# An encoder trunk in split fp32: the up projections take their k-tiles outside and the two token tiles inside

## The chip, the cores and the metric

The kernel runs on one core of a Trainium2 chip. A core has several engines, each with an instruction stream of its own that it works through in order: TensorE (PE in the profile) multiplies matrices into eight PSUM banks, VectorE (DVE) and ScalarE (ACT) work element by element, GpSimd (POOL) does little here, and SyncE (SP) issues the transfers from memory. The metric is the device time of one execution in microseconds. Durations in this text are of the profiled execution unless a sentence says otherwise.

## The reference

The program is a bidirectional encoder of two layers over 256 tokens of width 1024, in fp32:

```python
def swiglu(h, w_gate, w_up, w_down):
    return (jax.nn.silu(h @ w_gate) * (h @ w_up)) @ w_down
...
    for layer in range(DEPTH):
        h = rms_norm(x, ffn1_norm[layer])
        x = x + 0.5 * swiglu(h, ffn1_w_gate[layer], ffn1_w_up[layer], ffn1_w_down[layer])
        h = rms_norm(x, mix_norm[layer])
        ...
        h = rms_norm(x, ffn2_norm[layer])
        x = x + 0.5 * swiglu(h, ffn2_w_gate[layer], ffn2_w_up[layer], ffn2_w_down[layer])
    return rms_norm(x, final_norm)
```

The inner width of a SwiGLU is 2816. The line left out adds a mixer, an attention layer of one of two kinds, which the change doesn't touch.

## The kernel before

**Stages.** The kernel goes through six stages: SwiGLU (stage 0), the even mixer (1), SwiGLU (2), SwiGLU (3), the odd mixer (4), SwiGLU (5). The 256 tokens are two token tiles of 128, and the width is eight k-tiles of 128. The activations of a stage lie transposed in SBUF as `hT[tt][k]`.

**One product.** An fp32 product is made of three passes over split operands. ACT writes the rounded `hi` of a weight piece (L479), DVE the rest `lo` (L482), and PE does high by `hi` (L471), high by `lo` (L472) and low by `hi` (L473) in `mm`. A piece is 128 x 512 weights. A split of two pieces (128 x 1024) lives in one of seven `wp` buffers until PE has used both pieces with both token tiles. Weights arrive in three `raw` buffers of 1 MB; the next transfer is issued when the `lo` of the last split of a raw buffer is made.

**A SwiGLU stage** goes through five chunks of 512 inner columns (ci0 to ci4), a mixed chunk of 256, and then the down projection. An ordinary chunk makes the gate G and then the up projection U. `project` (L602) does one token tile at a time: it takes one PSUM bank and runs through the eight k-tiles, then the other token tile does the same with the same pieces. After the first of them ACT applies `silu` out of the bank; after U, DVE multiplies in `glu` (L677), which is what empties the bank. The result is turned by a DMA transpose (ACT copies L556 and L560 around it) and split for the down projection.

**Seven chunks.** Some chunks (`SEVEN`: ci2 of stages 0 and 5, ci1 and ci3 of stages 2 and 3) make G and U together by a Strassen scheme for some pairs of k-tiles: seven products for eight, named "1", "00", "01", "7", "5", "10", "6" in the order of the program. Of the four pairs of k-tiles the first one or two are done plainly, and then three or two by the scheme. Product "1" is the first to take a `pj` bank, "5" takes the other one. The weights of such a pair need more work on DVE: sums `two`, sums within `raw` (L395), and two splits `shi`/`slo` that have three buffers of their own. After the last product "1", ACT copies its bank (L766), and DVE combines the products (L769 to L812).

**Banks.** PSUM has 2 `pj` banks, 3 `s`, 1 `o` and 2 `tp`. U of a chunk ahead of a seven chunk uses the two `pj` banks.

**Order.** Every engine's instructions run in the order in which the program emits them. A counter (`tick`, one per product) sets that order: each tick adds a rate (`RATE`, `AHEAD_RATE` in the chunk ahead of a seven chunk, `SEVEN_RATE` within) to what is due, and when a split is due and a buffer is free (`room`), its `hi` and `lo` are emitted there. Tasks such as `glu` and `silu` wait for a number of ticks. So a split that is supplied earlier stands ahead of a `glu` that is emitted later, in the order of DVE and ACT.

**Down projection.** `DOWN` gives the order of its pairs (p plain, s Strassen); the last two pairs of the list are held to the end. When the last s pair has been issued, `combine` (L932 to L953) adds its products to `x`, ten operations on DVE, and `ENDS` sets the rate and what is due from there. Then `add_to_x` (L614) adds the plain part, and the next stage's transposes (L527) read `x`.

Of the kernel before, what the change touches and what calls it, by code (L numbers as in the profile page):

```python
# [20 lines left out]
NT = 2  # L21
# [10 lines left out]
FF_CHUNKS = [512, 512, 512, 512, 512]  # L32
# [14 lines left out]
DOWN_RATE = {0: 1.24, 2: 1.38, 3: 1.32, 5: 1.2}  # L47
ENDS = {0: [0.43, 0], 2: [0.4, 1], 3: [0.34, 0], 5: [0.26, 2]}
EVEN_RATE = [0.38, 0.48, 0.48, 0.48, 0.5]
# [41 lines left out]
}  # L91
AHEAD_RATE = {
    0: 0.81,
    2: 0.62,
    3: 0.55,
    5: 0.6,
}
SEVEN_RATE = {
# [107 lines left out]
class Trunk:  # L206
# [395 lines left out]
    def project(self, hT, pieces, tag):  # L602
# [4 lines left out]
        return ps  # L607

    def add_to_x(self, tt, sl, ps, scale, last=True):
        nxt = self.next  # L610
        if nxt.n < 6:
            yield 1
        x = self.x[tt][:, sl.start : sl.start + ps.shape[-1]]
        self.nc.vector.scalar_tensor_tensor(x, ps, scale, x, op0=ALU.mult, op1=ALU.add)  # L614
        if last:
            self.after(tt, sl, nxt)
# [42 lines left out]
    def ffn(self):  # L659
# [5 lines left out]
        tasks = []  # L665
# [7 lines left out]

        def glu(tt, f0, w, u, s):
            yield 1
            m = self.t([P, 512], "glu", 3)
            nc.vector.scalar_tensor_tensor(m[:, :w], u[:, :w], self.now.r[tt], s[:, :w], op0=ALU.mult, op1=ALU.mult)  # L677
            self.spawn(transposed(tt, f0, w, m), GLU_WAIT)
# [45 lines left out]
        sevens = SEVEN[self.now.n]  # L724
# [130 lines left out]
        f0 = 0  # L855
        self.spawn(x_sums())
        for ci, w in enumerate(FF_CHUNKS):
# [5 lines left out]

            tags = ["pj", "s", "s", "pj"] if ci - 1 in sevens else ["s", "s", "pj", "pj"]
            G = self.take(KD)
            S = []
            if self.now.n + ci == 0:
                both = self.first_gates(G)
            for tt in range(NT):
                g = both[tt] if self.now.n + ci == 0 else self.project(self.ready(tt), G, tags[tt])  # L870
                S.append(self.t([P, 512], "silu", SILUS[self.now.n]))
                self.start(silu(tt, w, g, S[tt]))
            U = self.take(KD)
            for tt in range(NT):
                u = self.project(self.now.hT[tt], U, tags[NT + tt])
                tasks.append(self.start(glu(tt, f0, w, u, S[tt])))
            f0 += w // P
# [688 lines left out]
```

## Time and profile before

| | |
|---|---|
| median of 3 runs | 943.91 us (942.9 to 944.78) |
| profiled execution | 942.41 us, span 940.6 us, granted clock 0.999 |
| PE busy | 921.9 us (98%) |
| DVE busy | 782.9 us (83%) |
| ACT busy | 677.8 us (72%) |
| stage 0, stage 1 | 0 to 187 us, 187 to 277 us |
| stage 2, stage 3 | 277 to 457 us, 457 to 638 us |
| stage 4, stage 5 | 638 to 757 us, 757 to 940 us |

The span runs from the first to the last instruction. In a row of the timeline stand the start, the busy time, the engine, the line, the operation with out<-in, and in brackets the idle time of the engine just before it with what ended it. PE, DVE and ACT overlap one operation with the next, so the distance between two starts is what an operation costs in a row of them.

### The profile page before, as it was taken

What the parts mean: (1) busy time and instruction counts of PE and PEld (TensorE: products, weight loads), DVE (VectorE), ACT (ScalarE), POOL (GpSimd) and SP (SyncE); (2) the same over time, 40 slices, a digit from 0 to 9 for tenths busy, and PEclk for the clock granted to TensorE, in tenths of its full rate; (3) what the DMA queues carried; (4) which work ended last, traced back from release to release, by engine and by line L of the source; (5) the groups of instructions that cost most, each with busy time, mean ns of one, the idle gap of its engine ahead of it and who ended that gap; (6) DMA issues with size and microseconds to landing.
All of it is one profiled execution on the core that took longest, in us unless ns stands there. A gap on an engine that the chain in (4) does not pass through costs nothing.

```text
span 940.6 us, 12391 instructions
## 1 busy us (share of the span) xinstructions
PE 921.9 (98%) x4399; PEld 752.7 (80%) x4399; DVE 782.9 (83%) x1212; ACT 677.8 (72%) x1091; POOL 92.5 (10%) x152
## 2 busy tenths in 40 slices
PE   9999999999999999999999999999999999999997
PEld 6887888877878788888888878778878788878886
DVE  6799778778869989888978897999767687986997
ACT  7678975477787778875657778657877577768753
POOL 1300000064410000000100000008030000000001
PEclk9999999999999999999999999999999999999999
DMA  8857875554326577766467777565534458487761
GB/s 297 282 166 247 250 234 194 182 152 106 101 91 201 205 231 233 236 212 250 152 179 228 194 239 224 210 244 172 164 106 136 134 178 247 139 253 217 230 224 45
DMA packets 129343, 183.16 MB, mean 195 GB/s; under 512 B 50688, under 2 KB 63744, under 8 KB 129280
## 3 DMA queue, kind: packets, MB, share of 16 engines
q1 hardware_dynamic: 128704, 181.58, 60.9%
q8 instruction: 34, 0.56, 0.2%
q10 hardware_dynamic: 576, 0.79, 0.2%
q14 instruction: 29, 0.24, 0.1%
HBM read 169.76 MB, written 1.05 MB: 182 GB/s over the span
## 4 chain that ended last, share of the span: by engine, by line
PE 66%; DVE 16%; ACT 10%; DMA 4%; issue 3%; POOL 0%; SPq 0%; POOLq 0%; ACTq 0%; DVEq 0%
PE pj L471 9%; PE pj L472 9%; PE pj L473 9%; PE s L472 9%; PE s L473 9%; PE s L471 9%; DVE lo L482 7%; ACT hi L479 3%; DMA glu<-turned 2%; ACT turned L560 2%; DVE raw L395 2%; PE o L1040 2%; ACT shi L479 2%; PE tp L1117 1%; PE o L473 1%
## 5 line engine op out<-in xcount | busy, mean ns | idle before, releaser
L482 DVE TENSOR_TENSOR lo<-raw,hi 128x1024 fp32r<-128x1024 f32 (+1 forms) x372 | 375.9, 1030 | 80.8 <-ACT hi L479 79.3
L479 ACT ACTIVATE hi<-raw 128x1024 fp32r<-128x1024 f32 (+1 forms) x372 | 318.4, 889 | 49.9 <-PE pj L473 12.2
L471 PE MATMUL pj<-hi,th 128*128 128x512 f32 x367 | 146.7, 400 | 0.9 <-ACT glu L766 0.9
L472 PE MATMUL s<-lo,th 128*128 128x512 f32 x373 | 145.5, 390 | 0.9 <-DVE lo L482 0.7
L471 PE MATMUL s<-hi,th 128*128 128x512 f32 x373 | 146.2, 392 | 0.0
L472 PE MATMUL pj<-lo,th 128*128 128x512 f32 x367 | 143.9, 392 | 2.3 <-DVE lo L482 2.0
L473 PE MATMUL s<-hi,tl 128*128 128x512 f32 x373 | 145.3, 390 | 0.0
L473 PE MATMUL pj<-hi,tl 128*128 128x512 f32 x367 | 143.3, 390 | 0.0
L472 PEld LDWEIGHTS pj<-lo,th 128*128 128x128 f32 x367 | 69.1, 188 | 17.6 <-DVE lo L482 5.1
L472 PEld LDWEIGHTS s<-lo,th 128*128 128x128 f32 x373 | 70.0, 188 | 16.2 <-DVE lo L482 2.0
L473 PEld LDWEIGHTS s<-hi,tl 128*128 128x128 f32 x373 | 70.0, 188 | 14.6
L471 PEld LDWEIGHTS s<-hi,th 128*128 128x128 f32 x373 | 70.0, 188 | 14.3
L471 PEld LDWEIGHTS pj<-hi,th 128*128 128x128 f32 x367 | 69.0, 188 | 15.4 <-ACT glu L766 1.3
L473 PEld LDWEIGHTS pj<-hi,tl 128*128 128x128 f32 x367 | 68.9, 188 | 14.6
L491 POOL TENSOR_TENSOR rstd<-var,mhalf 128x1 f32<-128x1 f32 (+2 forms) x16 | 17.1, 1069 | 594.3 <-ACT th L512 315.3
L560 ACT COPY turned<-glu 128x1024 uint16<-128x1024 uint16 (+1 forms) x48 | 60.1, 1252 | 10.3 <-DMA glu<-turned 10.3
L556 ACT COPY turned<-glu 128x1024 uint16<-128x1024 uint16 (+1 forms) x48 | 46.3, 965 | 23.8 <-DVE glu L794 17.5
L479 ACT ACTIVATE shi<-raw 128x1024 fp32r<-128x1024 f32 x30 | 31.8, 1058 | 42.0 <-DVE raw L395 26.1
L471 PE MATMUL s<-hi,g_h 128*128 128x512 f32 (+1 forms) x131 | 51.3, 392 | 0.0
L473 PE MATMUL s<-hi,g_l 128*128 128x512 f32 (+1 forms) x131 | 50.9, 388 | 0.0
L472 PE MATMUL s<-lo,g_h 128*128 128x512 f32 (+1 forms) x131 | 50.8, 388 | 0.0
L482 DVE TENSOR_TENSOR slo<-raw,shi 128x1024 fp32r<-128x1024 f32 x30 | 36.7, 1222 | 9.9 <-ACT shi L479 9.5
(482 smaller groups left out, 1672.4 us busy)
## 6 DMA issues: line engine op xcount, KB each, us to landing
raw<-in_ffn_w_down SPq DMA_DIRECT2D x44, 1024.0 KB, 5.1
raw<-in_ffn_w_up SPq DMA_DIRECT2D x28, 1024.0 KB, 5.1
raw<-in_ffn_w_gate SPq DMA_DIRECT2D x26, 1024.0 KB, 5.2
raw<-in_ffn_w_gate SPq DMA_DIRECT2D x35, 512.0 KB, 3.9
raw<-in_ffn_w_up SPq DMA_DIRECT2D x32, 512.0 KB, 4.9
raw<-in_odd_w_qkv SPq DMA_DIRECT2D x12, 1024.0 KB, 5.8
raw<-in_even_w_in SPq DMA_DIRECT2D x4, 1024.0 KB, 5.0
raw<-in_even_w_out SPq DMA_DIRECT2D x8, 512.0 KB, 5.9
```

The lines of the kernel that those rows point to most:

```text
L395: add = lambda o, x, y: self.nc.vector.tensor_tensor(o, x, y, op=ALU.add)
L471: mm(ps, h, wh, start=first, stop=False)
L472: mm(ps, h, wl, start=False, stop=False)
L473: mm(ps, l, wh, start=False, stop=last)
L479: self.nc.scalar.activation(hi, src, AF.Copy)
L482: self.nc.vector.tensor_tensor(lo, src, hi.bitcast(F32), op=ALU.subtract)
L491: nc.gpsimd.tensor_tensor(r[:, :n], v[:, :n], self.mhalf[:, :n], op=ALU.pow)
L556: self.nc.scalar.copy(planes.rearrange("p (h c) -> p h c", h=2), back.rearrange("p (c h) -> p h c", h=2))
L560: self.nc.scalar.copy(planes.rearrange("p (c h) -> p h c", h=2), back.rearrange("p (h c) -> p h c", h=2))
L1040: self.nc.tensor.matmul(O[64 * s : 64 * s + 64, i * P : i * P + P], v(b0 + i, s, kc), pT[s][:, i, kc, :], start=(kc == 0), stop=(kc == 1),)
L1117: nc.tensor.transpose(tb[:, o : o + P], p[:, i, kc * P : kc * P + P], self.ident)
```

## The change

A new function `project_both` takes both PSUM banks at the start and runs over the k-tiles outside and the two token tiles inside, so that a weight piece is used with both token tiles at once, and both banks are complete only at the end. It is used for U of all ordinary chunks but ci4 and the chunk between two seven chunks (ci2 of stages 2 and 3), which is U of ci0, ci1 and ci3 in stages 0 and 5 and of ci0 in stages 2 and 3; and for G of ci1 and ci4 in stages 0 and 5 (G of ci0 in stage 0 was done that way before). The two `glu` tasks of such a U wait 1 and 3 ticks. `AHEAD_RATE` goes from 0.62, 0.55 and 0.6 to 0.7, 0.65 and 0.75 in stages 2, 3 and 5. In stage 3 the Strassen pair s6 of the down projection changes places with the plain pair p1, and what is due after it starts at 3 and not at 0.

```diff
-    3: "p0 p2 s5 s3 p4 s8 p10 p1 s6 p9 p7",
+    3: "p0 p2 s5 s3 p4 s8 p10 s6 p1 p9 p7",
...
-ENDS = {0: [0.43, 0], 2: [0.4, 1], 3: [0.34, 0], 5: [0.26, 2]}
+ENDS = {0: [0.43, 0], 2: [0.4, 1], 3: [0.34, 3], 5: [0.26, 2]}
...
-AHEAD_RATE = {
-    0: 0.81,
-    2: 0.62,
-    3: 0.55,
-    5: 0.6,
-}
+AHEAD_RATE = {0: 0.81, 2: 0.7, 3: 0.65, 5: 0.75}
...
+    def project_both(self, pieces, tags):
+        ps = [self.bank(tag) for tag in tags]
+        n = len(pieces)
+        for k in range(n):
+            for tt in range(NT):
+                self.mm(ps[tt], self.now.hT[tt][k], pieces[k], k == 0, k == n - 1)
+        return ps
...
-        def glu(tt, f0, w, u, s):
-            yield 1
+        def glu(tt, f0, w, u, s, wait=1):
+            yield wait
...
-            tags = ["pj", "s", "s", "pj"] if ci - 1 in sevens else ["s", "s", "pj", "pj"]
+            behind = ci - 1 in sevens
+            tags = ["pj", "s", "s", "pj"] if behind else ["s", "s", "pj", "pj"]
+            apart = ci + 1 == len(FF_CHUNKS) or behind and ci + 1 in sevens
             G = self.take(KD)
-            S = []
+            S, both = [], None
             if self.now.n + ci == 0:
                 both = self.first_gates(G)
+            elif ci and not behind:
+                both = self.project_both(G, tags[:NT])
             for tt in range(NT):
-                g = both[tt] if self.now.n + ci == 0 else self.project(self.ready(tt), G, tags[tt])
+                g = both[tt] if both else self.project(self.ready(tt), G, tags[tt])
                 S.append(self.t([P, 512], "silu", SILUS[self.now.n]))
                 self.start(silu(tt, w, g, S[tt]))
             U = self.take(KD)
+            both = None if apart else self.project_both(U, tags[NT:])
             for tt in range(NT):
-                u = self.project(self.now.hT[tt], U, tags[NT + tt])
-                tasks.append(self.start(glu(tt, f0, w, u, S[tt])))
+                u = both[tt] if both else self.project(self.now.hT[tt], U, tags[NT + tt])
+                tasks.append(self.start(glu(tt, f0, w, u, S[tt], 1 + 2 * tt if both else 1)))
```

After the change the lines of the file stand elsewhere: `hi`, `lo` and the three passes are L474, L477 and L466 to L468, `glu` is L680, the transpose's copies are L551 and L555, and `add_to_x` is L617.

The first place is DVE in stage 0, around the two `glu` of ci1, which empty the two `pj` banks that the seven chunk ci2 takes next. Before, the first of them (of bank `pj_104`) stands further up, and the second here, at its end:

```order
L395 TENSOR_TENSOR two_112_550<-raw_91_468 128x1024
L677 SCALAR_TENSOR_TENSOR glu_116_572<-pj_104_521,rstd_37_213,silu_92_472 128x512
L482 TENSOR_TENSOR g1_0_l_115_570<-turned_88_459,g1_0_h_114_569 128x512
L482 TENSOR_TENSOR lo_118_579<-raw_91_468,hi_117_578 128x1024
L395 TENSOR_TENSOR raw_91_468<-two_112_550,raw_91_468 128x512
L395 TENSOR_TENSOR raw_91_468<-raw_91_468 128x512
L482 TENSOR_TENSOR slo_120_588<-two_112_550,shi_119_587 128x1024
L482 TENSOR_TENSOR slo_122_598<-raw_91_468,shi_121_597 128x1024
L482 TENSOR_TENSOR lo_125_607<-raw_100_503,hi_124_606 128x512
L395 TENSOR_TENSOR two_126_613<-raw_100_503 128x1024
L677 SCALAR_TENSOR_TENSOR glu_132_628<-pj_113_565,rstd_48_258,silu_103_520 128x512
```

The same place on DVE after the change, where ci1's banks are `pj_104` and `pj_105`:

```order
L477 TENSOR_TENSOR slo_119_583<-raw_91_466,shi_118_582 128x1024
L477 TENSOR_TENSOR lo_124_595<-raw_99_501,hi_123_594 128x512
L390 TENSOR_TENSOR two_125_601<-raw_99_501 128x1024
L477 TENSOR_TENSOR g1_0_l_122_592<-turned_94_477,g1_0_h_121_591 128x512
L477 TENSOR_TENSOR lo_127_611<-raw_99_501,hi_126_610 128x1024
L390 TENSOR_TENSOR raw_99_501<-two_125_601,raw_99_501 128x512
L390 TENSOR_TENSOR raw_99_501<-raw_99_501 128x512
L477 TENSOR_TENSOR slo_129_623<-two_125_601,shi_128_622 128x1024
L680 SCALAR_TENSOR_TENSOR glu_134_633<-pj_104_519,rstd_37_213,silu_102_517 128x512
L680 SCALAR_TENSOR_TENSOR glu_135_641<-pj_105_520,rstd_48_258,silu_103_518 128x512
```

Both `glu` now stand behind the first Strassen pair of ci2 and most of the second; before, the first stood ahead of the first pair's own `slo`.

The second place is ACT at the end of the same seven chunk, from the copy of product "1" to the `hi` of the last pieces of G of ci3. Before:

```order
L766 ACTIVATE glu_162_755<-pj_138_664 128x512
L560 COPY turned_137_658<-glu_132_628 128x2x512
L704 ACTIVATE quarters_150_714<-turned_137_658 128x128
L479 ACTIVATE hi_165_770<-raw_144_690 128x1024
L479 ACTIVATE g1_4_h_167_778<-turned_137_658 128x384
L479 ACTIVATE hi_169_787<-raw_144_690 128x1024
```

The same place on ACT after the change:

```order
L769 ACTIVATE glu_159_748<-pj_137_661 128x512
L555 COPY turned_136_655<-glu_134_633 128x2x512
L704 ACTIVATE quarters_161_760<-turned_136_655 128x256
L474 ACTIVATE g0_4_h_162_762<-turned_136_655 128x512
L474 ACTIVATE hi_165_767<-raw_144_690 128x1024
L555 COPY turned_141_668<-glu_135_641 128x2x512
L707 ACTIVATE quarters_161_760<-turned_141_668 128x128
L474 ACTIVATE hi_167_780<-raw_144_690 128x1024
```

The work on the first token tile's turned result has moved down to here, and one `turned` copy now stands between the two `hi`.

The third place is DVE at the end of stage 3, from the held pairs' last `lo` to the first sum into `x` (bank `o`) that the next stage's transposes read. Before:

```order
L482 TENSOR_TENSOR lo_1362_5953<-raw_1343_5848,hi_1361_5952 128x1024
L482 TENSOR_TENSOR lo_1365_5971<-raw_1353_5897,hi_1364_5970 128x512 x2
L482 TENSOR_TENSOR lo_1367_5983<-raw_1353_5897,hi_1366_5982 128x512 x2
L482 TENSOR_TENSOR lo_1370_5997<-raw_1358_5925,hi_1369_5996 128x512 x2
L939 SCALAR_TENSOR_TENSOR x0_84<-pj_1306_5717,x0_84 128x512
L942 SCALAR_TENSOR_TENSOR silu_1372_6017<-tp_1318_5756,silu_1371_6011 128x512
L945 SCALAR_TENSOR_TENSOR glu_1373_6022<-tp_1311_5735,silu_1372_6017 128x512
L948 SCALAR_TENSOR_TENSOR silu_1374_6027<-s_1312_5739,silu_1372_6017 128x512
L936 TENSOR_TENSOR x0_84<-x0_84,silu_1374_6027 128x512
L953 SCALAR_TENSOR_TENSOR glu_1375_6033<-s_1312_5739,glu_1373_6022 128x512
L614 SCALAR_TENSOR_TENSOR x0_84<-o_1283_5617,x0_84 128x512
```

The same place on DVE after the change, where `combine` follows `lo_1365` directly, from the last of its first five operations on:

```order
L944 TENSOR_TENSOR x0_84<-x0_84,silu_1369_5989 128x512
L477 TENSOR_TENSOR lo_1372_5997<-raw_1353_5903,hi_1371_5996 128x512
L961 SCALAR_TENSOR_TENSOR glu_1370_5995<-s_1312_5739,glu_1368_5984 128x512
L477 TENSOR_TENSOR lo_1372_5997<-raw_1353_5903,hi_1371_5996 128x512
L944 TENSOR_TENSOR x1_85<-x1_85,glu_1368_5984 128x512
L944 TENSOR_TENSOR x1_85<-x1_85,glu_1370_5995 128x512
L477 TENSOR_TENSOR lo_1375_6020<-raw_1358_5925,hi_1374_6019 128x512 x2
L617 SCALAR_TENSOR_TENSOR x0_84<-o_1283_5617,x0_84 128x512
```

`combine` starts four `lo` earlier, but those four (of the odd mixer's weights) and the two sums into `x1` now stand ahead of the sum from bank `o`.

## The prediction

> **What bounds the kernel now.** I read the page's busy times first, then TensorE's waits, then VectorE around the seven chunks, then the chain of waits there.
>
> ```profile
> PE 921.9 (98%) x4399; PEld 752.7 (80%) x4399; DVE 782.9 (83%) x1212; ACT 677.8 (72%) x1091; POOL 92.5 (10%) x152
> ```
>
> PE is busy for 921.9 of 940.6 us and the change leaves its 4399 matmuls as they are. So a gain can only come out of 18.7 us, and what PE waits for by name is less (line, releaser, us in all, times, longest):
>
> ```profile
> PE tp L527 <- DVE x L614: 2.1, 1, 2.1
> PE pj L472 <- DVE lo L482: 2.0, 3, 0.9
> PE s L472 <- DVE slo L482: 0.9, 2, 0.4
> PE tp L472 <- DVE slo L482: 0.8, 1, 0.8
> PE s L472 <- DVE lo L482: 0.7, 2, 0.5
> ```
>
> Waits for weights (`lo`, `slo`) come to 2.0 + 0.9 + 0.8 + 0.7 = 4.4 us, and the end of stage 3 (L527) to 2.1. Of stage 0, the windows of U of ci1 and of the seven chunk ci2 show, after stretch and length, busy PE, PEld, DVE, ACT:
>
> ```profile
> 41.50:52.20 10.70, 10.70 (x49) 8.87 (x48) 6.89 (x8) 8.89 (x10) 3.26 (x12) 1.00 0.92 310
> 52.20:72.20 20.00, 20.00 (x90) 16.41 (x89) 19.50 (x23) 15.28 (x18) 0.00 (x0) 1.00 0.47 135
> ```
>
> DVE has 3.8 us free in U and 0.5 in the seven chunk; PE waits for none of it until G of ci3. A piece that is released after two products, not after the other token tile's eight, frees its buffer earlier, so DVE can work ahead in U. Whether that helps is in the chain of waits (start, us, engine, line):
>
> ```profile
> 61.15 0.24 PE pj L473
> 61.47 1.07 ACT shi L479
> ...
> 71.04 0.48 ACT glu L766
> 71.52 1.27 ACT turned L560
> ...
> 73.12 0.96 ACT hi L479
> ...
> 76.58 1.23 DVE lo L482
> 77.85 0.50 PE pj L472
> ```
>
> The wait at 77.85 goes back without a gap in DVE and ACT to 61.47, where a `shi` waits for PE: product "5" of the first pair frees its buffer. PE starts that chain. Work done sooner ahead of 61 us can't shorten it; a PE that comes later lengthens it.
>
> **The change, part by part.**
>
> *Stage 0, the bank.* U of ci1 now ends both banks at 52.4, and both `glu` stand on DVE behind the first Strassen pair and most of the second. Product "1" takes the first bank here:
>
> ```profile
> 57.82 0.39 PE L471 MATMUL pj<-hi,th 128*128 128x512 f32 x1
> ```
>
> When is that `glu` done? Prices on DVE are distances between starts:
>
> ```profile
> 46.53 1.23 DVE L482 TENSOR_TENSOR lo<-raw,hi 128x1024 fp32r<-128x1024 f32 x1 [2.22 <-ACT hi L479]
> 47.67 0.69 DVE L482 TENSOR_TENSOR g_l<-turned,g_h 128x512 fp32r<-128x512 f32 x1
> 48.28 0.69 DVE L482 TENSOR_TENSOR lo<-raw,hi 128x512 fp32r<-128x512 f32 x1
> 48.88 1.22 DVE L395 TENSOR_TENSOR two<-raw 128x1024 f32<-128x1024 f32 x1
> 50.01 0.74 DVE L677 SCALAR_TENSOR_TENSOR glu<-pj,rstd,silu 128x512 f32<-128x512 f32 x1
> 50.68 0.68 DVE L482 TENSOR_TENSOR g_l<-turned,g_h 128x512 fp32r<-128x512 f32 x1
> ...
> 52.41 0.68 DVE L395 TENSOR_TENSOR raw<-two,raw 128x512 f32<-128x512 f32 x1
> ...
> 53.74 1.22 DVE L482 TENSOR_TENSOR slo<-two,shi 128x1024 fp32r<-128x1024 f32 x1
> ```
>
> A wide `lo`, `slo` or `two` costs 1.14, a narrow `lo` or `g_l` 0.6, the two `raw` sums 1.33 (52.41 to 53.74), `glu` 0.67. The row at 46.53 had waited for its `hi`, and on ACT:
>
> ```profile
> 42.00 1.06 ACT L479 ACTIVATE hi<-raw 128x1024 fp32r<-128x1024 f32 x1 [3.15 <-DMA raw<-in_ffn_w_up]
> ...
> 44.88 0.67 ACT L672 ACTIVATE silu<-s,rstd 128x512 f32<-128x512 f32 x1
> 45.45 1.57 ACT L479 ACTIVATE hi<-raw 128x1024 fp32r<-128x1024 f32 x2
> ```
>
> The first of these `hi` waits for a transfer that isn't sooner now. Then come two `silu` (0.57 each) and the second `hi` (0.95), so that `lo` starts at 42.0 + 0.95 + 1.14 + 0.95 = 45.1. From there to the end of the first `glu` stand, by the order, `lo`, narrow `lo`, `two`, `lo`, sums, `slo`, `g_l`, `slo`, narrow `lo`, `two`, `g_l`, `lo`, sums, `slo`, `glu`: 8 x 1.14 + 4 x 0.6 + 2 x 1.33 + 0.67 = 14.85. The bank is free at 59.9, and **PE waits 2.1 us** at 57.82. Bounds: 1.1 if the `silu` don't stand in the way, 2.8 if a `shi` behind two turned copies on ACT holds DVE by 0.7 more. None of it is covered: all later products stand behind that one.
>
> *Stage 0, the way out.* The chain from 61.47 starts later by those 2.1, and its tail is longer. On ACT, from the copy (71.04), there now stand two turned copies and, besides, these:
>
> ```profile
> 65.28 0.42 ACT L701 ACTIVATE quarters<-turned 128x256 f32<-128x256 f32 x1
> 65.61 0.62 ACT L479 ACTIVATE g_h<-turned 128x512 fp32r<-128x512 f32 x1
> ```
>
> Copy 0.48, turned copy and its quarters 1.6 (71.52 to 73.12), `g_h` 0.5, `hi` 0.98, turned copy and quarters 1.6, `hi` 0.98, `lo` 1.27 make 7.4, against 6.8 (71.04 to 77.85) before: 0.6 more. Stage 0 loses 2.1 + 0.6 = **2.7 us** (1.7 to 3.4). The smallest of the three waits in the 2.0 us group, at most (2.0 - 0.93)/2 = 0.5 with the largest quoted below, lies in U of ci0; it may go, but the transfer at 42.0 sets the bank's time in either case, so nothing of it stays.
>
> A rule bears on this. DVE's rows show the first `glu` at 50.01, while PE still works into the other bank. The Trainium skill, "Perfetto Trace Analysis", section "Optimizing Tensor Performance", wants independent groups to rotate through banks so that emptying one overlaps the next group's matmuls. K outside gives that up for the two token tiles; were the overlap worth nothing, the sum would be 2.1 us lower here and 1.3 lower in stage 5.
>
> *Stage 5* has the same shape:
>
> ```profile
> 806.67 0.39 PE L471 MATMUL pj<-hi,th 128*128 128x512 f32 x1
> ...
> 826.84 0.50 PE L472 MATMUL pj<-lo,th 128*128 128x512 f32 x1 [0.93 <-DVE lo L482]
> ```
> ```profile
> 819.79 0.57 ACT L766 ACTIVATE glu<-pj 128x512 f32<-128x512 f32 x1
> ```
>
> In stage 0 U of ci1 began 16.3 us ahead of product "1" (41.50 to 57.82, 72 matmuls), so here at 790.3. Here the buffers limit how far DVE runs ahead: the seventh split after U's first needs that one's buffer, which is free after 12 matmuls, at 790.3 + 2.7 = 793.0. Then on DVE and ACT by turns: `hi` 0.95, `lo` 1.14, sums 1.33; on ACT `shi` 0.96, turned copy and quarters 1.6, narrow `hi` 0.5, `g_h` 0.5, turned copy and quarters 1.6, `g_h` 0.5, `hi` 0.96; on DVE `lo` 1.14, sums 1.33, `g_l` and small ones 1.0, `slo` 1.14, `glu` 0.67: 808.3, a wait of 1.6. Without that buffer's wait it is 0.8, and if DVE isn't held by ACT none; I take 1.3. The tail by the stage 0 prices is 7.4 against 826.84 - 819.79 = 7.05, so **1.7 us** (0 to 2.2).
>
> *Stages 2 and 3, seven chunks.* In stage 2 ci1 is the seven chunk, and before, the second `glu` of ci0 and a `g_l` ran here:
>
> ```profile
> 301.42 0.74 DVE L677 SCALAR_TENSOR_TENSOR glu<-pj,rstd,silu 128x512 f32<-128x512 f32 x1
> ...
> 312.24 0.68 DVE L482 TENSOR_TENSOR g_l<-turned,g_h 128x512 fp32r<-128x512 f32 x1
> ```
> ```profile
> 305.46 0.39 PE L471 MATMUL pj<-hi,th 128*128 128x512 f32 x1
> ...
> 319.44 0.50 PE L472 MATMUL tp<-slo,k14h 128*128 128x512 f32 x1 [0.79 <-DVE slo L482]
> ```
>
> Ahead of the first `glu` now stand a `slo`, a narrow `lo` and a `two` more than ahead of the second before (2.9), and one `glu` less (0.7): it ends at 302.1 + 2.2 = 304.3. Its bank is wanted at 305.5, so PE doesn't wait. The `g_l` of 312.24 moves behind the third pair's `two`; that is 0.6 more ahead of the `slo` that ends the wait at 319.44, less what starts sooner: **0.4 us** (-0.3 to 1.0; 2.9 if that `glu` slips past 305.5). In the other seven chunks DVE's order ahead of the waits is the same, or nothing waited: 0 (-0.5 to 0.5). The same holds for G of ci1 and ci4 and U of ci3, whose banks are long free: 0.
>
> *End of stage 3.*
>
> ```profile
> 605.67 4.63 DVE L482 TENSOR_TENSOR lo<-raw,hi 128x1024 fp32r<-128x1024 f32 x4
> ...
> 628.32 0.68 DVE L939 SCALAR_TENSOR_TENSOR x<-pj,x 128x512 f32<-128x512 f32 x1
> ...
> 632.16 0.68 DVE L614 SCALAR_TENSOR_TENSOR x<-o,x 128x512 f32<-128x512 f32 x1
> ```
> ```profile
> 632.89 0.66 PE L527 MATMUL tp<-mats,x 128*128 128x128 f32 x4 [2.06 <-DVE x L614]
> ```
>
> `combine` starts four `lo` earlier, but the sum from `o` stands behind all of it and two more `lo`. The second of the four `lo` ends at 607.9; s6 takes `lo`n, `two`, `lo`, sums, two `slo` = 6.5, and at 614.4 the last held pair's transfer is issued (5.1 in the page, so 619.6); two `hi`, then two `lo` end at 622.9; two narrow `lo` 1.2, and twelve operations of 0.64 ((632.16 - 628.32)/6) bring the sum to 631.7, **0.5 us** sooner, of which I count 0.4 (-0.6 to +1.5, later transfers or none).
>
> Sum: 2.7 + 1.7 + 0.4 - 0.4 = +4.4 us. The profiled execution has 942.4 (span 940.6 and 1.8 around it), so 946.8. It lies 1.5 below the median of the runs, 943.9, to which I add the same: **948.3 us**.
>
> **Rivals.**
> A, working ahead wins. If DVE reaches the first `glu` of stage 0 by 57.8, 2.1 us sooner than my sum, PE never waits for a bank, and with buffers that come free sooner the waits for weights (4.4) go; the longer tails stay (0.6 and 0.4): -3.4, 940.5. For it: 3.8 us of free DVE in U. Against: the chain at 61.47 starts at PE.
> B, it washes out: the first bank is waited for about 1 us in one stage, and the end of stage 3 pays for it: +0.5, 944.4. For it: every stall lies in work that the change doesn't remove.
> C, slower by more: the first `glu` of stage 2 slips too (2.9 in place of 0.4) and both stages wait at their upper ends (3.4 + 2.2): +8, 952. It decides once DVE is 1.1 us later there than my sum.
>
> **How the numbers follow.** Forecast 0.5, A 0.22, B 0.2, C 0.08. Its own range is 945.5 to 951; to hold the time 8 times in 10, with A and B, 940 to 951.5. What a measurement of this kernel can tell from no change is 0.2%, 1.9 us. Faster: A, 0.22. Same: B and a little of the forecast's low end, 0.22. Slower: 0.56.
>
> **What would show it.** A wait of PE for DVE's `glu` at product "1" of ci2 in stages 0 and 5, near 2 us and 1.3; the wait at G of ci3 still there, ended by `lo`, its chain starting at a PE product again; L527's wait near 1.6. No `glu` row among PE's waits, or G of ci3 without a stall, would make the prediction wrong; so would stage 2's stalls gone.

## The result: slower by 1%, the waits came where they were expected and longer

The changed kernel takes **952.05 us** (median of 4 runs, 951.21 to 954.12), the kernel before 943.4 in the same comparison (942.23 to 944.78): a ratio of 1.0096, 95% interval 1.0083 to 1.011. The forecast was 948.3 with a range up to 951.5, so the side was right and the loss, 9 us of span, about twice the 4.4 of the sum.

TensorE's work is the same. This is the row of busy times after the change; the span is 949.6 us, 9.0 more than before.

```profile
PE 922.1 (97%) x4399; PEld 752.2 (79%) x4399; DVE 786.4 (83%) x1212; ACT 676.3 (71%) x1091; POOL 91.9 (10%) x152
```

The view of PE's waits after the change (line, releaser, us in all, times, longest) has a new row at its head, `glu`, and the wait at the end of stage 3, now L522, is 0.3 shorter:

```profile
PE pj L466 <- DVE glu L680: 5.5, 2, 3.3
PE pj L467 <- DVE lo L477: 3.6, 5, 0.8
PE tp L522 <- DVE x L617: 1.8, 1, 1.8
PE s L467 <- DVE slo L477: 1.7, 3, 0.8
PE s L467 <- DVE lo L477: 1.5, 3, 1.1
```

The timeline of DVE after the change shows what stands ahead of the first `glu` in stage 0 (start, us, engine, line, out<-in, and in brackets the idle time before with what ended it):

```profile
44.60 1.83 DVE L477 TENSOR_TENSOR lo<-raw,hi 128x1024 fp32r<-128x1024 f32 x2 [0.84 <-ACT hi L474]
...
51.09 0.68 DVE L477 TENSOR_TENSOR g_l<-turned,g_h 128x512 fp32r<-128x512 f32 x1
52.77 1.23 DVE L477 TENSOR_TENSOR slo<-raw,shi 128x1024 fp32r<-128x1024 f32 x1 [1.00 <-ACT shi L474]
...
58.72 1.22 DVE L477 TENSOR_TENSOR slo<-two,shi 128x1024 fp32r<-128x1024 f32 x1
59.85 1.40 DVE L680 SCALAR_TENSOR_TENSOR glu<-pj,rstd,silu 128x512 f32<-128x512 f32 x2
```

and the timeline of PE shows who waits for it, product "1" of ci2 in stage 0 and in stage 5:

```profile
57.08 0.39 PE L468 MATMUL o<-hi,tl 128*128 128x512 f32 x1
60.74 0.47 PE L466 MATMUL pj<-hi,th 128*128 128x512 f32 x1 [3.28 <-DVE glu L680]
...
814.60 0.50 PE L466 MATMUL pj<-hi,th 128*128 128x512 f32 x1 [2.21 <-DVE glu L680]
```

U of ci1 is finished near 51.9, but the `glu` that empties its banks starts at 59.85, behind everything DVE was given first. PE takes its work in order, and everything later stands behind that product.

G of ci3 still stalls. The rows of ACT from the copy of product "1" on, and the two PE rows that end the stall:

```profile
73.97 0.57 ACT L769 ACTIVATE glu<-pj 128x512 f32<-128x512 f32 x1
74.44 1.35 ACT L555 COPY turned<-glu 128x1024 uint16<-128x1024 uint16 x1
...
76.67 1.05 ACT L474 ACTIVATE hi<-raw 128x1024 fp32r<-128x1024 f32 x1
77.62 1.32 ACT L555 COPY turned<-glu 128x1024 uint16<-128x1024 uint16 x1
...
79.03 0.50 PE L467 MATMUL pj<-lo,th 128*128 128x512 f32 x1 [0.75 <-DVE lo L477]
81.54 0.50 PE L467 MATMUL pj<-lo,th 128*128 128x512 f32 x1 [0.77 <-DVE lo L477]
```

In that G PE loses 2.22 us against the steady distance of 0.227 us between starts, where it lost 1.49 before; in stage 5 it is 2.21 against 1.64. In stage 2, 300 to 330 us, PE's waits were 0.8 (`slo`, into a `tp` bank) and 0.5 (`lo`) before; now the same view reads

```profile
PE s L467 <- DVE lo L477: 1.1, 1, 1.1
PE tp L467 <- DVE slo L477: 0.8, 1, 0.8
PE s L467 <- DVE slo L477: 0.6, 1, 0.6
```

The length of each stage, from its first product to the next stage's, read off the timelines of the profiled executions (us; the runs below are in the same table, since most of them are read from it):

| | 0 | 1 | 2 | 3 | 4 | 5 | span | median, ratio to before |
|---|---|---|---|---|---|---|---|---|
| before | 179.9 | 90.5 | 179.0 | 181.7 | 118.8 | 183.8 | 940.6 | |
| after | 183.9 | 90.5 | 180.2 | 182.2 | 118.9 | 187.3 | 949.6 | 952.05, 1.0096 |
| e1 U of ci1 apart | 179.6 | 90.5 | 180.5 | 181.6 | 118.9 | 184.8 | 943.2 | 944.94, 1.0011 |
| e2 old rates | 185.5 | 90.5 | 179.8 | 184.1 | 118.8 | 185.6 | 951.5 | 952.25, 1.008 |
| e3 new rates alone | 180.1 | 90.5 | 180.5 | 183.3 | 118.8 | 184.8 | 945.2 | 945.86, 1.0019 |
| e4 new down order alone | 180.2 | 90.5 | 179.0 | 181.6 | 118.8 | 183.8 | 940.7 | 942.27, 0.9979 |
| e5 pause in the supply | 180.3 | 90.5 | 180.2 | 181.9 | 118.8 | 185.0 | 943.6 | 945.56, 1.0017 |
| e6 banks taken later | 181.1 | 90.5 | 180.2 | 182.1 | 118.9 | 185.6 | 945.4 | 947.28, 1.0034 |
| e7 U of ci1 alone | 188.9 | 90.5 | 178.9 | 181.9 | 118.8 | 185.9 | 951.9 | 954.1, 1.01 |
| e8 pause, sooner turn | 178.0 | 90.5 | 181.7 | 184.0 | 118.8 | 182.5 | 942.6 | 941.42, 0.9976 |
| e9 parts that help | 178.0 | 90.5 | 179.3 | 181.1 | 118.9 | 182.5 | 937.5 | 938.93, 0.9947 |
| e10 before, turn sooner | 181.4 | 90.5 | 179.1 | 182.0 | 118.8 | 184.6 | 943.6 | 945.52, 1.0019 |
| e11 before, turn later | 179.8 | 90.5 | 179.1 | 181.8 | 118.9 | 183.8 | 940.5 | 943.48, 0.9996 |
| e12 the same, new down order | 179.6 | 90.4 | 178.8 | 182.2 | 118.8 | 183.8 | 940.6 | 942.33, 0.9986 |

The 9.0 us are 3.9 in stage 0, 3.4 in stage 5, 1.25 in stage 2 and 0.5 in stage 3, less 0.3 by which the first product starts sooner. In the profiled executions of e2, e3 and e8 the granted clock is at 0.50 for 3.41 us where stage 3 ends (the last section), and their stage 3 is about 1.5 us longer for it; the changed kernel and the one before have no such drop in theirs.

### The profile page after: what moved, and what is told of

It reads as the page before. It is cut to its first block, busy times and chain, and to the rows that moved or that the text cites. A ratio compares the mean times of both kernels' runs of the same rounds, so it can differ in the third digit from the quotient of the medians.

```text
span 949.6 us, 12388 instructions
## 1 busy us (share of the span) xinstructions
PE 922.1 (97%) x4399; PEld 752.2 (79%) x4399; DVE 786.4 (83%) x1212; ACT 676.3 (71%) x1091; POOL 91.9 (10%) x152
## 4 chain that ended last, share of the span: by engine, by line
PE 60%; DVE 17%; ACT 11%; issue 5%; DMA 5%; POOL 1%; SPq 0%; POOLq 0%; ACTq 0%; DVEq 0%
PE pj L466 8%; PE pj L467 8%; PE pj L468 8%; PE s L466 8%; PE s L468 8%; PE s L467 8%; DVE lo L477 7%; ACT hi L474 4%; ACT turned L555 3%; DMA glu<-turned 2%; DVE two L390 2%; DVE raw L390 2%; PE o L1048 2%; PE tp L1125 1%; DMA raw<-in_ffn_w_up 1%
## 5 line engine op out<-in xcount | busy, mean ns | idle before, releaser
L477 DVE TENSOR_TENSOR lo<-raw,hi 128x1024 fp32r<-128x1024 f32 (+1 forms) x372 | 379.5, 1039 | 75.2 <-ACT hi L474 74.1
L474 ACT ACTIVATE hi<-raw 128x1024 fp32r<-128x1024 f32 (+1 forms) x372 | 318.5, 889 | 45.3 <-PE s L468 12.7
L466 PE MATMUL pj<-hi,th 128*128 128x512 f32 x367 | 147.0, 401 | 6.4 <-DVE glu L680 5.5
L466 PE MATMUL s<-hi,th 128*128 128x512 f32 x373 | 146.3, 392 | 0.5 <-ACT hi L474 0.4
L468 PE MATMUL s<-hi,tl 128*128 128x512 f32 x373 | 145.3, 390 | 0.0
L468 PE MATMUL pj<-hi,tl 128*128 128x512 f32 x367 | 143.3, 390 | 0.0
L466 PEld LDWEIGHTS pj<-hi,th 128*128 128x128 f32 x367 | 69.0, 188 | 22.2 <-issue 4.7
L466 PEld LDWEIGHTS s<-hi,th 128*128 128x128 f32 x373 | 70.0, 188 | 15.3 <-ACT hi L474 0.6
L468 PEld LDWEIGHTS s<-hi,tl 128*128 128x128 f32 x373 | 70.0, 188 | 14.6
L468 PEld LDWEIGHTS pj<-hi,tl 128*128 128x128 f32 x367 | 68.9, 188 | 14.5
L551 ACT COPY turned<-glu 128x1024 uint16<-128x1024 uint16 (+1 forms) x48 | 46.0, 968 | 31.1 <-DVE glu L797 20.0
L555 ACT COPY turned<-glu 128x1024 uint16<-128x1024 uint16 (+1 forms) x48 | 60.1, 1251 | 10.7 <-DMA glu<-turned 10.5
L474 ACT ACTIVATE shi<-raw 128x1024 fp32r<-128x1024 f32 x30 | 31.7, 1058 | 43.6 <-DVE raw L390 25.6
L477 DVE TENSOR_TENSOR slo<-raw,shi 128x1024 fp32r<-128x1024 f32 x30 | 36.7, 1224 | 21.2 <-ACT shi L474 20.7
L466 PE MATMUL s<-hi,g_h 128*128 128x512 f32 (+1 forms) x131 | 51.4, 392 | 0.0
L468 PE MATMUL s<-hi,g_l 128*128 128x512 f32 (+1 forms) x131 | 50.9, 388 | 0.0
```

What stands on the lines that cost most here:

```text
L466: mm(ps, h, wh, start=first, stop=False)
L468: mm(ps, l, wh, start=False, stop=last)
L474: self.nc.scalar.activation(hi, src, AF.Copy)
L477: self.nc.vector.tensor_tensor(lo, src, hi.bitcast(F32), op=ALU.subtract)
L551: self.nc.scalar.copy(planes.rearrange("p (h c) -> p h c", h=2), back.rearrange("p (c h) -> p h c", h=2))
L555: self.nc.scalar.copy(planes.rearrange("p (c h) -> p h c", h=2), back.rearrange("p (h c) -> p h c", h=2))
```

## The experiments

**Who makes the `glu` late?** The theory is the prediction's: with both token tiles inside, both `glu` are emitted behind splits that DVE was given earlier, and the bank comes free late. The rival is that the new rates of supply crowd DVE. Two runs start from the changed kernel and undo one each. The first does U of the chunks ahead of a seven chunk one token tile at a time:

```diff
-            apart = ci + 1 == len(FF_CHUNKS) or behind and ci + 1 in sevens
+            apart = ci + 1 == len(FF_CHUNKS) or ci + 1 in sevens
```

> The changed kernel, but U of a chunk that stands ahead of a seven chunk (ci1 in stages 0 and 5, ci0 in stages 2 and 3) is made one token tile after the other again; all else of the change stays. Queue theory (the loss is the wait of product 1 for a bank whose glu stands on VectorE behind supplied splits, and the longer tail behind it): no wait of TensorE for a glu is left, stages 0 and 5 end as before (within 0.5 us), the end of stage 3 gains 0.3, and what is left is at most 1.8 in the seven chunks of stages 2 and 3: 943.5 to 945.5 where before has 943.4. Rate theory (AHEAD_RATE puts too much work ahead in stages 2, 3 and 5): stage 0 comes back, stages 2, 3 and 5 stay: 947 to 949. Theory that k outside itself and G of both tiles cost (late silu, buffers): still above 947, with waits at G of ci1 or in U of ci3.

Measured: 944.94 us, ratio 1.0011 (1.0002 to 1.002), as the theory said. The first two rows of its view of PE's waits, where the `glu` of DVE is gone:

```profile
PE pj L467 <- DVE lo L477: 2.3, 3, 0.9
PE tp L522 <- DVE x L617: 1.7, 1, 1.7
```

So 6.4 of the 9.0 us of span go back with U of the chunks ahead of a seven chunk, and the two waits of 3.28 and 2.21 with them. Stage 2 doesn't come back (180.5 us). The second run undoes the rates:

```diff
-AHEAD_RATE = {0: 0.81, 2: 0.7, 3: 0.65, 5: 0.75}
+AHEAD_RATE = {0: 0.81, 2: 0.62, 3: 0.55, 5: 0.6}
```

> The changed kernel with the old AHEAD_RATE of 0.62, 0.55 and 0.6 in stages 2, 3 and 5. Queue theory: stage 0 keeps its 3.7 us; in stage 5 the first glu stands one slo (1.14) further up, so that the wait of 2.4 becomes 1.2; the seven chunks of stages 2 and 3 may gain up to 1: 949.5 to 951. Rate theory: stages 2, 3 and 5 come back but for 0.5: 946 to 947.

Measured: 952.25 us, ratio 1.008 (1.0063 to 1.0096), above both forecasts. The rates are not what costs stage 0. In stage 5 they have a part: the wait fell from 2.2 to 0.4 us, and 1.6 of its 3.4 us went back. But stage 0, whose program is that of the changed kernel, was 1.7 us longer still. The timeline of this run shows why:

```profile
57.54 0.39 PE L468 MATMUL o<-hi,tl 128*128 128x512 f32 x1
61.41 0.77 PE L466 MATMUL pj<-hi,th 128*128 128x512 f32 x1 [3.48 <-DVE glu L680]
...
62.82 0.63 PE L466 MATMUL s<-hi,th 128*128 128x512 f32 x1
63.25 0.63 PE L467 MATMUL s<-lo,th 128*128 128x512 f32 x1
```

Behind a wait of 3.48 us the matmuls stand 0.43 us apart, and not 0.23 as at 61 us of the changed kernel: the granted clock dropped to 0.50. The last section comes back to it.

**The other parts alone.** Two runs start from the kernel before and add one part: the rates (the line above, the other way round), and the order of stage 3's down projection with its due count.

> The kernel before with the new AHEAD_RATE (0.7, 0.65, 0.75 in stages 2, 3, 5) and nothing else of the change. With up apart and the new rates, stage 2 lost 1.5 us, stage 3 nothing and stage 5 0.9. If the rates do that, they do it here too: stage 0 as before, stage 2 +1.5, stage 5 +0.9, 945.5 to 946.5. If these came from G of both tiles and U of ci0 and ci3: 943.5 to 944.5.

Measured: 945.86 us, ratio 1.0019 (1.0011 to 1.0028), as forecast. Stage 2 is 1.5 us longer, as in e1, and stage 5 1.0. The prediction had put stage 2's loss down to the loop, with its moved `g_l`. The new rates cost it with the old loop, and e2, with the new loop and the old rates, is still 0.8 longer there (179.8): either alone costs it, and the two don't add up (1.25 in the changed kernel). Which of the splits that are supplied sooner costs it wasn't followed further.

The other run has the new order alone:

```diff
-    3: "p0 p2 s5 s3 p4 s8 p10 p1 s6 p9 p7",
+    3: "p0 p2 s5 s3 p4 s8 p10 s6 p1 p9 p7",
...
-ENDS = {0: [0.43, 0], 2: [0.4, 1], 3: [0.34, 0], 5: [0.26, 2]}
+ENDS = {0: [0.43, 0], 2: [0.4, 1], 3: [0.34, 3], 5: [0.26, 2]}
```

> The kernel before with the new order and end of stage 3's down projection and nothing else of the change. By the prediction's step: L527's wait for x 2.06 becomes 1.6, stage 3 gains 0.3 to 0.5, 943 to 944 where before has 943.4 to 944.5: not to be told from no change in the time, but in the rows. Rival: s6 moved up waits for its own slo (0.5 or more) and the gain is lost.

Measured: 942.27 us, ratio 0.9979 (0.997 to 0.9988): faster, by more than was expected (943 to 944). In the profiled execution the wait at L527 is 0.4 shorter:

```profile
PE tp L527 <- DVE x L614: 1.7, 1, 1.7
```

The span is none the shorter, 940.7 against 940.6. The timed executions of the kernel before lie in two groups, near 943 and near 944.6, and those of this kernel nearly all in the lower one. The granted clock goes with the groups: of the 90 executions of the kernel before that were timed beside these experiments, 54 of the 55 from 944 us up have a mean of 0.996 or 0.997, and 18 of the 26 below 943.5 have 0.998 or 0.999. This fits one drop of the clock more, like the one that e3 and e8 have at the end of stage 3, and an order of the down projection that makes it rarer. It isn't shown for the kernel before, since its profiled execution is one of the lower group; and the last run below, which has the new order too, spreads from 941.5 to 944.9.

**Can both token tiles inside be had without the wait?** Two cures, both on top of the changed kernel. Either DVE is given nothing that stands ahead of the `glu` (no split is supplied in the last three k-tiles of U of ci1 in stages 0 and 5):

```diff
+PAUSE = 3
...
+    def project_both(self, pieces, tags, pause=0):
...
+            if k == n - pause:
+                self.rate = 0
```

> The changed kernel, in which the supply pauses during the last three of the eight k-tiles of U of ci1 in stages 0 and 5, so that the glu of both banks stand ahead of the next splits on VectorE; loops, banks and rates stay. Queue theory: in stage 0 the first glu ends near 55 and no wait for it is left in stage 0 or 5 (2.9 and 2.4 us gone); the longer tail (0.6 and 0.4) and the 1.8 of stages 2 and 3 stay: 946 to 947.5. Theory that VectorE has too much to do whatever the order: the wait moves to a lo or slo in the seven chunk and the time stays near 952.

or PE asks for the banks later (in the first Strassen pair of stages 0 and 5, products "1" and "5" come last):

```diff
+                late = first and self.now.n in (0, 5)
+                if not late:
+                    product("1", h[0][k + 1], b11, first, last)
...
+                if late:
+                    product("1", h[0][k + 1], b11, first, last)
+                    product("5", K[2][j], t5, first, last)
```

> The changed kernel, in which products 1 and 5 of the first Strassen pair stand behind the other five in stages 0 and 5, so that the banks are wanted 3.4 us later; VectorE's order stays as in the changed kernel. Queue theory: no wait for glu in stage 0 (bank free at 60.6, wanted at 60.7), at most 0.3 in stage 5; but product 5 frees its shi buffer 1.4 us later than in the old order, so that the chain behind it starts 0.7 to 1.1 later than before and stages 0 and 5 lose 1.3 and 1.6 in place of 3.7 and 3.4: 947.5 to 948.5. Theory that VectorE is late whatever waits: 951 to 952, the wait at G of ci3 longer by what the bank's wait was.

Measured: 945.56 us, ratio 1.0017 (1.0008 to 1.0026), and 947.28 us, ratio 1.0034 (1.0021 to 1.0046), both a little below what the queue theory gave. Neither has a row for DVE's `glu` among PE's waits, so the queue on DVE is the cause, and moving either end of it is a cure. In the timeline of the pause, PE waits for neither bank, since the first `glu` stands here:

```profile
53.96 0.74 DVE L683 SCALAR_TENSOR_TENSOR glu<-pj,rstd,silu 128x512 f32<-128x512 f32 x1
...
70.63 0.57 ACT L772 ACTIVATE glu<-pj 128x512 f32<-128x512 f32 x1
71.10 1.35 ACT L556 COPY turned<-glu 128x1024 uint16<-128x1024 uint16 x1
...
73.32 1.04 ACT L475 ACTIVATE hi<-raw 128x1024 fp32r<-128x1024 f32 x1
74.27 1.32 ACT L556 COPY turned<-glu 128x1024 uint16<-128x1024 uint16 x1
```

It isn't faster than before, because the other term of the sum, the longer tail at G of ci3, is still there: two turned copies stand around the first `hi`, and PE loses 2.24 us in G of ci3 of stage 0 and 2.50 in stage 5 (2.54 and 2.62 with the banks taken later). Stage 2's 1.2 us are still there too.

**The wait alone.** From the kernel before, only U of ci1 of stages 0 and 5 gets both token tiles inside, at the old rates:

```diff
+            both = self.project_both(U, tags[NT:]) if ci == 1 and self.now.n in (0, 5) else None
```

> The kernel before with k outside only in U of ci1 in stages 0 and 5, old rates, nothing else. Queue theory: nearly the whole loss of the change from this alone: wait for glu 2.9 in stage 0 (with the tail 3.6) and about 1.3 in stage 5 (with the tail 1.8): 948.5 to 950. Theory that the loss needs G of ci1 made that way too, or U of ci0 (whose two glu come late): under 946.

Measured: 954.1 us, ratio 1.01 (1.0087 to 1.0113), slower than the whole change. In stage 0 the wait is there, and longer than expected; in stage 5, where 1.3 was expected, there is none:

```profile
PE pj L471 <- DVE glu L685: 4.1, 1, 4.1
```

Stage 0 is 9 us longer, of which the wait is 4.1. The view of PE's busy time by stretches (length, busy PE, PEld, DVE, ACT, POOL, then the granted clock) shows the rest:

```profile
62.00:64.00 2.00, 1.82 (x4) 1.50 (x5) 0.69 (x2) 1.93 (x2) 0.00 (x0) 0.50 0.00 0
64.00:66.00 2.00, 2.00 (x6) 1.59 (x5) 0.00 (x0) 0.06 (x1) 0.00 (x0) 0.50 0.82 160
```

From 62 to 68 us PE runs 4 to 6 matmuls in 2 us, where it runs 10 or 11 at the full clock in the changed kernel; against the distance of 0.227 us that costs 2.9 us. The tail at G of ci3 takes 0.7, and U of ci3, one token tile at a time here, loses 1.07 waiting for weights: together with the wait 8.8. In stage 5 the 2.1 us are the tail (0.6) and U of ci3 (1.57). So in stage 0 the size was off and not the place, and a wait cost more than its length once the clock followed it; stage 5 lost about what was expected, elsewhere.

**The tail.** If the turned copies make the stall at G of ci3, the first of them has to go elsewhere. On top of the pause, the first token tile's copy comes after 9 products and not 16:

```diff
+            soon = tt == 0 and f0 == 4 and self.now.n in (0, 5)
+            tb = yield from self.turned_over(m, w, SOON if soon else TURN_WAIT[1])
```

> The kernel with the pause, in which also the turned copy of the first token tile of ci1 is read back 7 ticks sooner in stages 0 and 5, so that it stands on ScalarE ahead of the third pair's shi and not between the copy of product 1 and the last hi of G of ci3. If the tail is what still costs in stages 0 and 5: the stall of G of ci3 goes from 2.24 to 1.5 in stage 0 and from 2.50 to 1.7 in stage 5, 944 to 945. If not: as the kernel with the pause, 945.6.

Measured: 941.42 us, ratio 0.9976 (0.9966 to 0.9986), better than expected: stage 0 is 1.9 us shorter than before, stage 5 1.3, and no stall is left at G of ci3. Stage 2 is 2.7 us longer than before: 1.2 as in the changed kernel and 1.5 at its end, where the transposes now wait 1.31 us for a sum into `x`. Stage 3 has the drop of the clock. So the next run keeps stages 0 and 5 of this one and the new order of the down projection, and gives stages 2 and 3 their old rates and loops back:

```diff
+AHEAD_RATE = {0: 0.81, 2: 0.62, 3: 0.55, 5: 0.75}
...
+            apart = ci + 1 == len(FF_CHUNKS) or self.now.n in (2, 3)
```

> This keeps of the change what the runs so far showed to cost nothing or to help: both token tiles inside in stages 0 and 5, with no split supplied in the last three k-tiles of U of ci1 and the first token tile's turned copy after 9 products instead of 16; stage 3's order of the down projection. Stages 2 and 3 go back to one token tile at a time and to the old rates of supply, 0.62 and 0.55. Theory (the stages add up, the rates are what cost stages 2 and 3): stages 0 and 5 as in the run with the sooner turn, 178.0 and 182.5 us, stages 2 and 3 as before, 179.0 and 181.4: a span near 937 and a median of 939 to 940.5, a ratio near 0.996. Rival (what a stage gains is given back by the next, whose transfers come no sooner): 941 to 943, no better than the run with the sooner turn, with stages 1, 2 or 3 longer by what stage 0 gains.

Measured: **938.93 us**, ratio 0.9947 (0.9936 to 0.9959), the fastest kernel here: the stages add up, but for 0.3 us that stage 2 gives back at its end. The profiled spans differ by 3.1 us (937.5 and 940.6) and the medians by 5.2, because the median of the kernel before lies in its upper group; so some 2 of the 5 us seem to be the clock's. In its timeline the `glu` stands at 54.51, PE takes the bank at 57.71 without a wait, and on ACT the `hi` stands directly behind product 1's copy:

```profile
54.51 0.74 DVE L684 SCALAR_TENSOR_TENSOR glu<-pj,rstd,silu 128x512 f32<-128x512 f32 x1
...
57.71 0.39 PE L468 MATMUL pj<-hi,th 128*128 128x512 f32 x1
...
70.78 0.58 ACT L774 ACTIVATE glu<-pj 128x512 f32<-128x512 f32 x1
71.26 1.05 ACT L476 ACTIVATE hi<-raw 128x1024 fp32r<-128x1024 f32 x1
72.21 1.34 ACT L557 COPY turned<-glu 128x1024 uint16<-128x1024 uint16 x1
```

**Does it need the k-tiles outside?** The order of ACT at that place can be had in the kernel before by the second token tile's turned copy alone. Twice one number is changed there, to 9 products and to 18 instead of 16.

> The kernel before, with one number changed: in ci1 of stages 0 and 5 the second token tile's turned copy comes after 9 products instead of 16. Theory (the sooner turn alone makes the gain at G of ci3, and the order of the k-tiles has no part in it): the copy of 71.42 us moves to about 66, the hi behind product 1's copy starts at once, and the 1.5 us of stage 0 and 1.6 of stage 5 at G of ci3 go: a median of 941 to 942, a ratio near 0.9975. Rival (it takes both token tiles inside as well, since here the second glu stands late and its copy would only hold the next shi): the copy delays the third pair's shi by up to 1.4 us, PE waits there for slo instead, and the time is 943.5 to 945.5.

Measured: 945.52 us, ratio 1.0019 (1.0009 to 1.0028): the rival holds. The stall at G of ci3 went, and this took its place, just ahead of that G:

```profile
66.53 1.35 ACT L561 COPY turned<-glu 128x1024 uint16<-128x1024 uint16 x1
67.74 1.06 ACT L480 ACTIVATE shi<-two 128x1024 fp32r<-128x1024 f32 x1
...
71.91 1.22 DVE L483 TENSOR_TENSOR slo<-raw,shi 128x1024 fp32r<-128x1024 f32 x1
...
73.18 0.50 PE L473 MATMUL s<-slo,th 128*128 128x512 f32 x1 [1.42 <-DVE slo L483]
```

The copy holds the `shi` behind it, and the small operations that follow the copy on DVE hold the `slo`, which before started 2.3 us earlier. U of ci3, where nothing was lost before, loses 0.8 us in stage 0 and 0.4 in stage 5 besides.

> The kernel before, with one number changed: in ci1 of stages 0 and 5 the second token tile's turned copy comes after 18 products instead of 16, so that on ACT the first hi of the last pieces of G of ci3 stands ahead of it and not behind it. This is the order that the run with the parts that help has there, with one token tile after the other as before. Theory (the gain at G of ci3 is a matter of what stands ahead of that hi on ACT and needs no k-tiles outside): the hi starts 1.6 us sooner, the lo behind it too, and most of the 1.5 us of stage 0 and 1.6 of stage 5 at G of ci3 go: 941 to 942.5, a ratio near 0.9975. Rival (with one token tile after the other the buffers come free too late for it, or the quarters that follow the later copy hold the next lo): the stall stays or moves on by one product, 943.5 to 945.

Measured: 943.48 us, ratio 0.9996 (0.9987 to 1.0005). ACT's order at the copy is now that of the fastest kernel, and its `hi` starts at 71.56, but nothing is gained: the rival holds again. The stall at G of ci3 is gone in both stages, and PE loses 0.98 us in U of ci3 of stage 0 and 1.46 in stage 5, where it lost nothing before:

```profile
71.09 0.57 ACT L768 ACTIVATE glu<-pj 128x512 f32<-128x512 f32 x1
71.56 1.05 ACT L480 ACTIVATE hi<-raw 128x1024 fp32r<-128x1024 f32 x1
...
86.70 0.50 PE L473 MATMUL s<-lo,th 128*128 128x512 f32 x1 [0.31 <-DVE lo L483]
...
837.56 0.50 PE L473 MATMUL s<-lo,th 128*128 128x512 f32 x1 [0.90 <-DVE lo L483]
```

In the fastest kernel DVE makes the `lo` for that U at nearly the same time (its rows at 85.12 and 86.85 against 85.43 and 87.16 here), and PE waits for none of them. What differs is how fast PE asks: with one token tile at a time a piece lasts PE 3 matmuls, 0.68 us, and the first token tile runs through all eight pieces in half of U; with both inside a piece lasts 6 matmuls, 1.36 us. This fits the 1.07 us that U of ci3 lost in e7, where it too ran one token tile at a time: in the changed kernel, with both inside and as long a stall in the G ahead of it (2.22 us, 2.21 in e7), it lost nothing. But a run that changes this U alone in the fastest kernel was not made, so that this is argued and not shown.

> The same, with the change's order of the third SwiGLU's down projection and what is due after it besides. No U has its k-tiles outside. Theory (gains add up, the k-tiles outside give nothing of their own): 939 to 940.5, as fast as the run with the parts that help. Rival (both token tiles inside are needed for the stages 0 and 5 of that run): 941 to 943, where the run before this one gains and this adds the 0.2% of the down projection's order alone, or less.

Measured: 942.33 us, ratio 0.9986 (0.9977 to 0.9995), 3.4 us above the fastest kernel and as fast as the new down order alone. So with the old loop neither place of the second turned copy that was tried had the gain of stages 0 and 5. With the new loop it came once the `glu` and a turned copy were moved with it (e8); which of the changed G and U it needs no run separates.

## Why the prediction was right or wrong

**Right: what sets the end, and the side.** Product "1" of ci2 waits for the `glu` in stages 0 and 5, the tail of the chain at G of ci3 is longer, and L522's wait is shorter by 0.3, where 0.4 was counted. That chain starts at a PE product again, as its steps after the change show:

```profile
64.20 0.24 PE pj L468
64.44 0.02 issue
64.46 1.07 ACT shi L474
```

e1, e5 and e6 show the mechanism of the bank from three sides.

**Wrong: four sizes, all in the same direction.**

- *Stage 0, the bank: 2.1, measured 2.9* (from 57.82 to 60.74). The step that failed is "PE waits 2.1 us", which left the wait of DVE for a `shi` behind two turned copies to the upper bound. It came, 1.00 us in the row at 52.77. The rest of the sum held: `lo` at 44.6 plus 14.85 plus 1.0 makes 60.45, and the first of the two `glu` ended near 60.5. The bound of 2.8 was the better value. PE itself came half a us sooner (it would have taken the bank at 57.31), which is why it sat idle for 3.28.
- *Stage 5, the bank: 1.3 (0 to 1.6), measured 2.2.* The step counted one missing buffer. DVE waited for a `hi` again and again there, four times for 0.9 to 1.4 us, and ACT's `hi` for PE; the first two such rows of DVE are

```profile
794.53 1.23 DVE L477 TENSOR_TENSOR lo<-raw,hi 128x1024 fp32r<-128x1024 f32 x1 [1.37 <-ACT hi L474]
...
796.82 0.69 DVE L477 TENSOR_TENSOR lo<-raw,hi 128x512 fp32r<-128x512 f32 x1 [1.06 <-ACT hi L474]
```

With the old rate the wait was 0.4 (e2): the rate, which the sum had passed over, decides it. U of ci3, counted at 0, lost 0.4 there besides.
- *Stage 2: 0.4, measured 1.25,* and *the second seven chunk of stage 3: 0 (up to 0.5), measured 0.8.* The step read the order of DVE and, in stage 2, put the loss down to a moved `g_l` and to the wait that ended at 319.44. That wait is no longer than before (0.8 in both views); the loss lies in the two waits for `slo` and `lo` ahead of it, 1.1 us. New rates alone (e3) and the new loop alone (e2) both bring it, and the sum had no term for the rates by themselves. Stage 3's loss doesn't come with the rates: e1 and e3 don't have it, e2 has 0.6 of it, so, as far as these runs tell, it goes with U of ci0, the only loop that changed in stages 2 and 3, where the step had counted on an unchanged order. How it gets there from U of ci0 stays open.
- *The tails: 0.6 and 0.4,* measured 0.73 and 0.57.

Together 4.4 became 9.0, and the median lies 0.55 us beyond the range. The range failed for the same reason: its upper end took each term's own bound, but nothing for several near theirs at once. Rival C gave the time, 952, by a mechanism that did not come: stage 2's `glu` did not slip, and PE waited for no bank there. The four timed runs of the changed kernel go from 951.2 and 951.35 at a mean granted clock of 0.997 and 0.999 to 954.1 at 0.995, so that drops of the clock may have had a part in the median. The profiled one, of 951.35, has no drop ahead of its end and yet the whole 9.0 us of span, so the sum would be as wrong without them.

**The rule on the banks.** The Trainium skill, "Perfetto Trace Analysis", section "Optimizing Tensor Performance", asked for groups that rotate through banks. By that rule, e1 agrees: with that U apart, the waits for a bank are gone. But the fastest kernel fills both banks together and waits for neither. Some 5 us of other products stand between the end of U (52.3) and the next use of a bank (57.7), and two `glu` at 0.7 us each have ample room there, as long as they aren't queued behind 7 us of other work on DVE, as they were in the changed kernel.

**Rival A** had a true part. The new loop does win 3 us in stages 0 and 5 (e9). It comes once the `glu` and a turned copy are moved, and, as far as e11 and e7 tell, from the slower demand for weights in U of ci3; whether work that DVE does early has a part in it no run separates.

## What to carry to other kernels

A loop turned inside out changes when results are complete, and with it where the operation that empties a bank stands in its engine's queue; read that queue before the loop is judged, and hold back what is supplied ahead of it. When a stall goes, look at the operation one step behind on the same engine, since e5, e10 and e11 each removed one stall and were left with another. A sum of small waits wants a term for every number that is changed, the rates too, and a range for all of them being late together.

## What the runs showed of the hardware

The clock was not expected to matter. A wait of TensorE of 3.28 us left it at 1.00, waits of 3.48 and 4.08 us were followed by 0.50. These are the stretches behind the wait, first in the changed kernel, where the clock is the number after POOL's:

```profile
62.00:64.00 2.00, 2.00 (x10) 1.66 (x9) 0.00 (x0) 0.62 (x1) 0.00 (x0) 1.00 0.59 113
```

and in the run with the old rates (e2):

```profile
62.00:64.00 2.00, 2.00 (x6) 1.61 (x5) 0.00 (x0) 1.29 (x2) 0.00 (x0) 0.50 0.22 45
```

The six executions of e2 run from 949.3 us at a mean granted clock of 0.998 to 953.3 at 0.995. The Trainium skill, "TensorE: Matmul & The Clock Gate", section "HAM oscillation — how this bites in real kernels", warns of idle gaps over about 3.4 us; these three waits agree with it. But other traces here differ, and the measurement decides: the clock also dropped behind shorter waits. In e8, at the end of stage 3, it is at 0.50 behind a wait of 2.18 us:

```profile
634.61 0.66 PE L524 MATMUL tp<-mats,x 128*128 128x128 f32 x4 [2.18 <-DVE x L621]
...
636.00:638.00 2.00, 2.00 (x6) 1.51 (x6) 1.38 (x5) 1.78 (x6) 0.00 (x0) 0.50 0.04 14
```

In e2 and e3 it dropped at the same place beside waits of 2.34 and 2.29 us, while e10 waited 2.57 there and stayed at 1.00. In e4, e5 and e6 it dropped near 545 us, behind a wait of 0.89 us and shorter ones just ahead of it. So the length of one wait doesn't decide alone, and what else does no run here settles. Each of these drops lasted 3.41 us, the one in e7 twice that, and the matmuls in it stand 0.43 us apart. From the first transposes of `x` to the next stage's first product e8 took 6.66 us and e3 6.52, where the kernel before took 5.07. So a wait can have two prices: here 3.3 us cost about 3.4, and 4.1 us cost 4.1 and 2.9 more.
